# Where the second projection of the keys' latent stands among the indexer's query tiles

## The chip, the cores and the metric

The program runs on one core of one Trainium2 chip. The metric is the time of one execution on the device, in microseconds (us), less is better. A core has a matmul engine (TensorE, in the profile PE, with its weight loads as PEld), a vector engine (VectorE, DVE), a scalar engine (ScalarE, ACT), GpSimd (POOL), and a queue (SyncE, SP) from which most transfers are issued. Each engine works through its own instructions strictly in the order in which they stand in the program, and waits for the others by semaphores.

## The reference

Two layers of a transformer block with 512 tokens and a width of 1024. A layer projects its input with one matrix of 13 x 128 columns and then runs two kinds of attention: eight heads of latent attention (MLA), whose keys and values come out of a 256 wide latent, and eight heads of sparse attention (DSA), where an indexer picks 128 keys for each query. After that come the output projection, a layer norm, a mixture of 16 experts with two per token, and another layer norm.

```python
proj = h @ w_in
qa, kva, kr, dq, dk, dv, iq, ik, iw = jnp.split(proj, SPLIT_POINTS, axis=-1)
# MLA: the keys' latent
c_kv = rms_norm(kva, kv_norm_g)
k_nope = (c_kv @ w_uk).reshape(B, T, MLA_HEADS, MLA_NOPE)
v = (c_kv @ w_uv).reshape(B, T, MLA_HEADS, MLA_V)
# DSA: the indexer
rel = jax.nn.relu(jnp.einsum('bthd,bsd->bths', iqb, ik) * (IDX_DIM ** -0.5))
score = jnp.einsum('bths,bth->bts', rel, iwb).astype(jnp.float32)
score = jnp.where(key_idx[None, None, :] <= tq[None, :, None], score, -jnp.inf)
_, sel = lax.top_k(score, n_keep)
```

## The kernel before, in words

The kernel takes the 13 column tiles of the first projection in a fixed order (S, two for the indexer's queries IQ, DKV, two for the keys' latent KVA, three for QA, four for DQ). Each tile is a `proj`: 24 matmuls of 128x512 into one PSUM bank, since the numbers are split into a high and a low part and three products are summed (`project`, L264 to L271). Before a tile can be multiplied its weights are split: ScalarE writes the high part (L163), GpSimd or VectorE the low part (L164). The banks for these products, and for scores, come from a ring of four named `mm`.

`latents(i)` (L333 to L336) is the projection of one of the two KVA tiles. ScalarE then reads its bank twice, once for the scaled latent `kvg` (L335) and once for its squares `sqk` (L336). GpSimd adds the two squares (L381, at the `anchor`), and TensorE sums them over the columns with four small matmuls (L418).

The indexer (L339 to L377) runs over the query tiles i = 1, 2, 3 (tile 0 needs no choice). For each of eight heads it does one matmul of the queries with the keys (L347), of 256, 384 or 512 columns for i = 1, 2, 3, then on ScalarE a relu that frees the bank (L352), then on VectorE one multiply-add into `acc` (L355 for head 0, L358 for heads 1 to 7). The queries of heads 0 to 3 and of heads 4 to 7 lie in two tiles `iq`, which come back through DRAM (`big<-iqd`). When all heads of a tile are summed, VectorE takes the 128 largest of each row in 16 rounds of a maximum of eight (L365) and a replacement (L366), then compares (L368) and writes the distance mask `dd` (L372). This top-k is given a lower priority (`LOWER`), so that the scheduler puts the rounds between other work of VectorE.

`KVA_AT` (L338) tells ahead of which (query tile, head) of the indexer the two `latents` are emitted; `proj` of the QA and DQ tiles follow the indexer. A scheduler orders the instructions of each engine from the order of emission, priorities and its own estimates; the order is fixed when the program is built. After QA and DQ come the norm factors (L422, L427, L434), the values (L457), and the attention heads in the groups of `HEADS`, "m0 m1d0 m2d1 m3d2 d3": m is a pair of latent heads, d a pair of sparse heads. A head is: four scores on TensorE (L545 for m, L558 and L559 for d), minimum with the mask on VectorE (L490), exponential on ScalarE (L492), reciprocal and scaling on VectorE (L494, L498), transposes on TensorE (L502) with copies on ScalarE (L504), and the product with the values (L511). A sparse head's fourth query tile needs the mask that tile i = 3 of the indexer makes. `queries` makes the queries of a pair of latent heads (24 matmuls named `mm<-qg,hl`, L220 to L223, then L530 on VectorE), `latent` the keys of a pair (six matmuls `mm<-big,hl`, then L536 and L537).

Of the kernel before, what the change touches and what calls it, by code (L numbers as in the profile page):

```python
# [95 lines left out]
def block_kernel(ctx, tc, xT0, x0, win, wqk, wuv, wo, gvec, lnp, rw, rb, wgu, wdn, consts, angles, stripd, rowsd, out):  # L96
# [56 lines left out]
    def ps(tag):  # L153
        return psp.tile([128, 512], F32, name=tag, bufs={"mm": 4, "tr": 2, "pv": 2}[tag])
# [76 lines left out]
    def attention(l, xh, xl, wraw, first, rest, x_dram):  # L231
# [101 lines left out]
        def latents(i):  # L333
            p = proj(T_KVA + i)
            nc.scalar.activation(kvg[i], p, AF.Copy, scale=gv[:, l, 3 + i:4 + i])  # L335
            nc.scalar.activation(sqk[i], p, AF.Square)  # L336

        KVA_AT = ((1,0), (3,0))  # L338
        for i in range(1, NT):  # L339
            n = 128 * (i + 1)  # L340
            acc, work = u4p("aw")
# [1 line left out]
            for h in range(8):  # L343
                if (i, h) in KVA_AT:
                    latents(KVA_AT.index((i, h)))
                p = ps("mm")
# [31 lines left out]
        for i in range(2):  # L378
            if KVA_AT[i] is None:
                latents(i)  # L380
# [1039 lines left out]
    for l in range(L):  # L1420
        r, pre = attention(l, xh, xl, wraw, ws, rest, src)
        y = experts(l, r, pre)
        wraw = pre["win"]
        new = combine(l, r, *y, pre["x1"], wraw)
        if l + 1 < L:
            xh, xl, rest, ws = new
        src = x1d
# [59 lines left out]
```

## Time and profile before

| what | us |
|---|---|
| median of 3 runs | 1191.95 (1191.82 to 1192.46) |
| the profiled execution, its own time | 1192.57 |
| its span, first to last instruction | 1190.8 |
| busy: PE, PEld, DVE, ACT, POOL | 1142.6, 893.5, 1020.2, 791.2, 285.6 |
| first layer, indexer from the first KVA tile's end to the first QA tile | 40.25 to 56.64 |
| second layer, the same | 628.24 to 647.35 |

Times within the trace count from the start of the span. The profiled execution lies 0.62 us above the median, and 1.77 us of its time lie outside the span. Over the whole span TensorE is busy 96% of the time and VectorE 86%, but those are means over stages with different limits: from about 42 to 146 us and again from about 637 to 737 us VectorE is the engine without gaps. Ends of matmuls are modelled in the profile, so a busy TensorE isn't always one at its peak; the weight loads beside it (PEld) tell more.

### The profile page before, as it was taken

To read this page: it belongs to the slowest core of one execution; us is meant where nothing else is said; L and a number is where in the kernel's file an instruction comes from. 1 tells how busy PE (TensorE), PEld (TensorE's weight loads), DVE (VectorE), ACT (ScalarE), POOL (GpSimd) and SP (SyncE) were. 2 spreads that over 40 slices of the span, in tenths; PEclk is the share of its full clock that TensorE was granted. 3 is DMA by queue.
4 is the path that set the end of the run, shared out by engine and by line. 5 is a ranking of instruction groups with operands and counts; after the bars stand their busy time and mean duration, and the time that the engine had idled before them with its cause. 6 is when DMAs were issued, how large, how long until landed. Compare 5 with 4: busy or idle time off the path is not lost. (4 is left out here: it accounts for less than half of the span.)

```text
span 1190.8 us, 16760 instructions
## 1 busy us (share of the span) xinstructions
PE 1142.6 (96%) x5705; PEld 893.5 (75%) x5705; DVE 1020.2 (86%) x1858; ACT 791.2 (66%) x1253; POOL 285.6 (24%) x236
## 2 busy tenths in 40 slices
PE   8999899999999999999998998999999999999996
PEld 6786555788788888887696765567887888888873
DVE  4599968399999999988957999774999999999898
ACT  4633668445888888887445346683468888888882
POOL 2345233121111111111132453422212111112011
PEclk9999999999999999999998999999999999999998
DMA  7626104366999999994735170144669999999841
GB/s 263 183 82 203 71 1 142 142 236 247 405 395 393 393 386 375 383 333 176 289 104 151 58 260 2 39 138 155 242 270 397 400 391 389 392 378 375 328 189 71
DMA packets 57547, 292.50 MB, mean 246 GB/s; under 512 B 10309, under 2 KB 14149, under 8 KB 29040
## 3 DMA queue, kind: packets, MB, share of 16 engines
q1 hardware_dynamic: 47664, 270.48, 60.9%
q0 software_dynamic: 8352, 15.66, 3.5%
q10 hardware_dynamic: 1440, 5.24, 1.1%
q8 instruction: 46, 0.75, 0.2%
q14 instruction: 45, 0.37, 0.1%
HBM read 267.96 MB, written 33.03 MB: 253 GB/s over the span
## 5 line engine op out<-in xcount | busy, mean ns | idle before, releaser
L163 ACT CAST hl<-big 128x1024 fp32r<-128x1024 f32 x438 | 457.4, 1054 | 123.0 <-PE mm L1065 51.3
L164 DVE TENSOR_TENSOR hl<-big,hl 128x1024 fp32r<-128x1024 f32 x403 | 483.7, 1227 | 47.7 <-ACT hl L163 41.7
L1064 PE MATMUL mm<-hl,xh 128*128 128x512 f32 x504 | 207.2, 411 | 0.6 <-ACT hl L163 0.6
L1065 PE MATMUL mm<-hl,xh 128*128 128x512 f32 x504 | 197.3, 392 | 0.0
L1086 PE MATMUL pv<-hl,hT 128*128 128x512 f32 x720 | 169.9, 390 | 0.1
L1086 PEld LDWEIGHTS pv<-hl,hT 128*128 128x128 f32 x720 | 134.7, 188 | 28.7 <-DVE hl L164 1.0
L271 PE MATMUL mm<-big,hl 128*128 128x512 f32 (+1 forms) x624 | 140.3, 384 | 2.4 <-ACT big L163 1.7
L271 PEld LDWEIGHTS mm<-big,hl 128*128 128x128 f32 x624 | 112.9, 193 | 27.7 <-ACT hl L163 2.3
L164 POOL TENSOR_TENSOR hl<-big,hl 128x1024 fp32r<-128x1024 f32 x35 | 86.5, 2476 | 133.7 <-ACT hl L163 118.2
L1028 POOL DMA_INDIRECT xg<-xdr,ii x30 | 54.0, 1800 | 268.9 <-DVE ii L1042 242.4
L1064 PEld LDWEIGHTS mm<-hl,xh 128*128 128x128 f32 x504 | 94.8, 188 | 16.8 <-ACT hl L163 1.1
L1065 PEld LDWEIGHTS mm<-hl,xh 128*128 128x128 f32 x504 | 95.1, 189 | 15.7
L1065 PE MATMUL mm<-hl,xl 128*128 128x512 f32 x252 | 98.9, 392 | 0.0
L1064 PE MATMUL mm<-hl,xl 128*128 128x512 f32 x252 | 98.8, 392 | 0.0
L635 PE MATMUL mm<-hl,big 128*128 128x512 f32 x384 | 93.4, 396 | 0.0
L492 ACT ACTIVATE P<-P,mn 128x128 f32<-128x128 f32 (+3 forms) x128 | 71.9, 569 | 17.2 <-DVE mn L490 14.8
L635 PEld LDWEIGHTS mm<-hl,big 128*128 128x128 f32 x384 | 70.8, 188 | 13.6
L1106 POOL DMA_INDIRECT ydr<-y,ii x28 | 30.2, 1079 | 189.4 <-ACT y L1102 117.5
L504 ACT COPY big<-tr 128x512 f32<-128x512 f32 (+3 forms) x128 | 49.8, 432 | 36.5 <-PE tr L502 35.6
L502 PE MATMUL tr<-cn,P 128*128 128x128 f32 x320 | 61.9, 293 | 9.1 <-DVE P L498 8.3
L502 PEld LDWEIGHTS tr<-cn,P 128*128 128x128 f32 x320 | 36.2, 141 | 41.7 <-ACT big L504 17.1
L572 POOL TENSOR_TENSOR mh<-dd,cn 128x256 f32<-128x256 f32 (+2 forms) x64 | 44.6, 718 | 64.9 <-DVE mn L490 39.5
(277 smaller groups left out, 1816.7 us busy)
## 6 DMA issues: line engine op xcount, KB each, us to landing
big<-wgu SPq DMA_DIRECT2D x128, 1024.0 KB, 8.2
big<-wdn SPq DMA_DIRECT2D x64, 1024.0 KB, 7.9
big<-win SPq DMA_DIRECT2D x10, 1024.0 KB, 5.4
ydr<-zz SPq DMA_DIRECT2D x2, 4096.0 KB
big<-wo SPq DMA_DIRECT2D x8, 1024.0 KB, 14.8
big<-ydr SPq DMA_DIRECT2D x8, 1024.0 KB, 12.7
big<-wqk SPq DMA_DIRECT2D x4, 1024.0 KB, 5.1
big<-dq SPq DMA_DIRECT2D x32, 128.0 KB, 2.3
```

The source lines that it names most:

```text
L163: i = nc.scalar.copy(hi, src).ins
L164: last_lo[0] = (eng or nc.vector).tensor_sub(lo, src, hi.bitcast(F32)).ins
L271: nc.tensor.matmul(p[:, ts], w[j == 1][:, k * 128:(k + 1) * 128], x, start=(j + k == 0), stop=(j == end and k == 7))
L492: nc.scalar.activation(e, e, AF.Exp, bias=mn[:, i:i + 1], scale=-1.0, accum_out=su[:, i:i + 1])
L502: nc.tensor.transpose(p[:, (i - kb) * 128:(i - kb + 1) * 128], P[:, PO[i] + kb * 128:PO[i] + (kb + 1) * 128], ident)
L504: copies.append(nc.scalar.copy(pt[kb], p[:, :512 - 128 * kb]).ins)
L572: last_mask[0] = nc.gpsimd.tensor_tensor(m[:, c:c + w], dd, C("slope", h, h + 1).to_broadcast([128, w]), op=OP.mult)
L635: R["pe"] = nc.tensor.matmul(pp[t][i], x, w[:, i * 512:(i + 1) * 512], start=first, stop=last).ins
L1028: return nc.gpsimd.indirect_dma_start(out=st[e]["xg"], out_offset=None, in_=xdr[l], in_offset=bass.IndirectOffsetOnAxis(ap=st[e]["ii"][:, ...
L1064: nc.tensor.matmul(pg, x, w[:, :512], start=(k == 0 and x is a and w is wh), stop=last)
L1065: nc.tensor.matmul(pu, x, w[:, 512:], start=(k == 0 and x is a and w is wh), stop=last)
L1086: nc.tensor.matmul(py[i], x, w[:, i * 512:(i + 1) * 512], start=(k == 0 and x is a and w is wh), stop=last)
```

## The change

The second `latents` is emitted ahead of head 4 of query tile 1 in place of head 0 of query tile 3. It holds for both layers. Nothing else differs in the source; the scheduler then orders much of the first half of the attention anew.

```diff
-        KVA_AT = ((1,0), (3,0))
+        KVA_AT = ((1, 0), (1, 4))
```

TensorE in the first layer, from the first KVA tile (24 matmuls L271) to the QA and DQ tiles; L347 are the indexer's scores and L418 the sums over the latent's squares:

```order
 L271 MATMUL mm<-big,hl 128x512 x24
-L347 MATMUL mm<-ik,big 128x256 x8
-L347 MATMUL mm<-ik,big 128x384 x8
+L347 MATMUL mm<-ik,big 128x256 x4
 L271 MATMUL mm<-big,hl 128x512 x24
-L347 MATMUL mm<-ik,big 128x512 x5
-L418 MATMUL pv<-cn,sqk 128x1 x4
-L347 MATMUL mm<-ik,big 128x512 x3
+L347 MATMUL mm<-ik,big 128x256 x4
+L347 MATMUL mm<-ik,big 128x384
+L418 MATMUL pv<-cn,sqk 128x1
```

The second 24 matmuls stood behind the scores of two query tiles and now stand behind four scores of the first; the sums L418 follow among the scores of tile 2.

The same place in the second layer:

```order
-L347 MATMUL mm<-ik,big 128x256 x8
+L347 MATMUL mm<-ik,big 128x256 x4
+L271 MATMUL mm<-big,hl 128x512 x24
+L418 MATMUL pv<-cn,sqk 128x1 x4
+L347 MATMUL mm<-ik,big 128x256 x4
 L347 MATMUL mm<-ik,big 128x384 x8
-L271 MATMUL mm<-big,hl 128x512 x24
```

Here all four sums L418 come directly behind the 24 matmuls, and the scores of heads 4 to 7 behind those.

VectorE in the first layer, in the attention, around the end of the last top-k, whose compare is L368 and whose masks are the two L372 (`mh` marks the first pair of sparse heads). Before:

```order
L490 ISA P,mn<-mm,mh 128x384
L490 ISA mn 128x1
L365 MAX m_640<-aw 128x8
L366 MATCH_REPLACE aw<-m_640,aw 128x512
L368 TENSOR_TENSOR aw<-aw 128x512
L530 TENSOR_TENSOR q<-mm,ct 128x512
L372 SCALAR_TENSOR_TENSOR dd<-aw,at 128x384
L372 SCALAR_TENSOR_TENSOR dd_325<-aw,at 128x128
L530 TENSOR_TENSOR q<-mm,ct 128x512
L490 ISA P,mn<-mm,mh 128x512
```

After the change:

```order
L490 ISA P,mn<-mm,mh 128x384
L490 ISA mn 128x1
L365 MAX m_637<-aw 128x8
L366 MATCH_REPLACE aw<-m_637,aw 128x512
L365 MAX m_640<-aw 128x8
L366 MATCH_REPLACE aw<-m_640,aw 128x512
L368 TENSOR_TENSOR aw<-aw 128x512
L372 SCALAR_TENSOR_TENSOR dd<-aw,at 128x384
L372 SCALAR_TENSOR_TENSOR dd_325<-aw,at 128x128
L490 ISA P,mn<-mm,mh 128x512
```

The L490 at the top is the first sparse head's in the first listing and the second sparse head's in the second: the three L490 of that second head, four L490 of a further latent head, both L530 and one L164 now stand ahead of the two L372.

TensorE in the first layer, where both orders have just issued the second sparse head's scores (L558, L559); L502 are transposes of finished heads:

```order
 L558 MATMUL mm<-kk,big 128x512
-L502 MATMUL tr<-cn,P 128x128
 L559 MATMUL mm<-kk,big 128x512
-L502 MATMUL tr<-cn,P 128x128 x6
 L220 MATMUL mm<-big,hl 128x512
 L221 MATMUL mm<-big,hl 128x512
 L220 MATMUL mm<-big,hl 128x512
-L502 MATMUL tr<-cn,P 128x128 x3
+L221 MATMUL mm<-big,hl 128x512
+L223 MATMUL mm<-big,hl 128x512 x2
+L545 MATMUL mm<-ke,q 128x128
+L545 MATMUL mm<-ke,q 128x256
```

The six matmuls of the next `latent` and its four scores L545 have moved ahead of the first transposes of the group with a sparse head.

## Rows read from the trace of the kernel before

**Rows 1.** Busy time by stretch: us, then busy us of PE, PEld, DVE, ACT, POOL.

```profile
46.60:134.70 88.10, 83.08 (x364) 62.83 (x364) 85.52 (x213) 37.83 (x75) 34.97 (x20) 0.98 0.40 132
637.20:725.70 88.50, 82.88 (x363) 62.61 (x363) 85.72 (x213) 38.17 (x76) 32.40 (x19) 0.98 0.39 131
57.00:87.00 30.00, 30.00 (x146) 25.05 (x145) 29.09 (x57) 10.96 (x16) 12.87 (x5) 1.00 0.25 89
148.30:215.00 66.70, 63.61 (x345) 40.13 (x345) 49.73 (x168) 49.54 (x154) 22.90 (x35) 0.97 0.25 85
739.40:806.00 66.60, 63.52 (x350) 39.97 (x350) 50.03 (x168) 49.95 (x156) 22.98 (x35) 1.00 0.27 89
```

**Rows 2.** Timeline of TensorE, first layer: start, us, instruction, count [idle before, releaser].

```profile
41.68 4.42 PE L347 MATMUL mm<-ik,big 128*128 128x256 f32 x13 [0.92 <-ACT sqk L336]
45.90 6.41 PE L271 MATMUL mm<-big,hl 128*128 128x512 f32 x24
...
56.64 27.55 PE L271 MATMUL mm<-big,hl 128*128 128x512 f32 x120
...
94.17 3.00 PE L434 MATMUL pv<-dg,cn 128*128 128x512 f32 x4 [1.80 <-POOL dg L427]
```

**Rows 3.** The same, second layer.

```profile
628.98 0.86 PE L347 MATMUL mm<-ik,big 128*128 128x256 f32 x4 [0.79 <-DMA big<-iqd]
632.84 4.12 PE L347 MATMUL mm<-ik,big 128*128 128x256 f32 x12 [2.99 <-DMA big<-iqd]
...
647.35 27.48 PE L271 MATMUL mm<-big,hl 128*128 128x512 f32 x120
```

**Rows 4.** Timeline of ScalarE, both layers.

```profile
41.52 5.38 ACT L352 ACTIVATE big<-mm 128x256 f32<-128x256 f32 x16
...
52.34 0.69 ACT L335 ACTIVATE kvg<-mm,gv 128x512 f32<-128x512 f32 x1 [4.52 <-PE mm L271]
52.93 0.59 ACT L336 ACTIVATE sqk<-mm 128x512 f32<-128x512 f32 x1
53.41 2.55 ACT L352 ACTIVATE big<-mm 128x512 f32<-128x512 f32 x5
...
630.24 1.22 ACT L352 ACTIVATE big<-mm 128x256 f32<-128x256 f32 x4
```

**Rows 5.** Timeline of GpSimd, first layer, the sum of squares.

```profile
53.60 1.28 POOL L381 TENSOR_TENSOR sqk<-sqk 128x512 f32<-128x512 f32 x1 [3.24 <-ACT sqk L336]
```

**Rows 6.** Timeline of VectorE, the first tile's sums and top-k, both layers.

```profile
42.53 4.01 DVE L358 SCALAR_TENSOR_TENSOR aw<-big,iwt,aw 128x256 f32<-128x256 f32 x7
...
633.15 4.03 DVE L358 SCALAR_TENSOR_TENSOR aw<-big,iwt,aw 128x256 f32<-128x256 f32 x7
```

**Rows 7.** Timeline of VectorE, first layer, in the attention.

```profile
112.62 0.68 DVE L530 TENSOR_TENSOR q<-mm,ct 128x512 f32<-128x512 f32 x1
...
141.96 0.75 DVE L372 SCALAR_TENSOR_TENSOR dd<-aw,at 128x384 f32<-128x384 f32 x2
...
144.61 0.29 DVE L490 CUSTOM_DVE_ANT_0 P<-mm,at 128x128 f32<-128x128 f32 x1
...
146.56 3.63 DVE L498 TENSOR_SCALAR P<-P,rc 128x128 f32<-128x128 f32 x4
...
153.15 1.22 DVE L164 TENSOR_TENSOR hl<-big,hl 128x1024 fp32r<-128x1024 f32 x1
```

**Rows 8.** Timeline of TensorE: the first head's scores, the first sparse transposes (both layers).

```profile
114.95 2.43 PE L545 MATMUL mm<-ke,q 128*128 128x128 f32 x8 [0.67 <-ACT ke L536]
...
148.26 0.30 PE L502 MATMUL tr<-cn,P 128*128 128x128 f32 x1 [1.07 <-DVE P L498]
739.40 0.30 PE L502 MATMUL tr<-cn,P 128*128 128x128 f32 x1 [1.07 <-DVE P L498]
```

**Rows 9.** Granted clock (the number behind POOL's count) in two stretches.

```profile
44.00:48.00 4.00, 4.00 (x12) 3.04 (x12) 3.46 (x9) 3.82 (x9) 0.05 (x1) 0.57 0.38 158
94.00:99.00 5.00, 4.83 (x10) 2.66 (x11) 4.79 (x13) 0.00 (x0) 5.00 (x4) 0.66 0.57 131
```

## The prediction

> **What bounds the kernel now.** I read the busy time by stretch first, since the page's means (TensorE 96%, VectorE 86%) hide which engine ends last where the change is. From 46.6 to 134.7 us in the first layer VectorE is busy 85.52 of 88.10 us, and the second layer repeats it with 85.72 of 88.50 [rows 1]. The 3% missing are the small gaps between an instruction and the one that needs its result. TensorE is nearly as busy there, but VectorE's time cannot be shortened: it is the three top-k of the indexer, its sums, and the first heads of the attention, one behind the other. The timelines then show where that stretch begins and where it is paid. It begins when the last sum of query tile 1 ends, at 42.53 + 4.01 = 46.5 us, and 633.15 + 4.03 = 637.2 us in the second layer [rows 6]; the first top-k follows at once. It is paid where TensorE wants to transpose the first group with a sparse head: it waits 1.07 us for VectorE's L498 there, in both layers [rows 8], and that L498 is behind the last top-k, whose masks (L372) end at 142.7 us [rows 7]. So until about 146 us the top-k chain on VectorE sets the time, and TensorE has little to spare at its end. What delays the first top-k delays everything after it, as far as no later slack takes it up.
>
> **The change, first layer.** It removes nothing and adds nothing. 24 matmuls move from behind 16 scores to behind four.
>
> TensorE's first part gets better. Head 3's score needs the bank that `sqk` frees, and runs at 41.7 as before [rows 2]. The projection needs head 0's bank, which ScalarE frees 0.4 us after 41.52 [rows 4], so it starts at 42.0. At 27.55/120 = 0.23 us a matmul [rows 2] it takes 5.5 us plus 0.2 for the last to drain: 47.7.
>
> Heads 4 to 7 come out later, and that is the core of it. ScalarE must read the projection's bank twice first, 0.59 to the next start and 0.48 more [rows 4]: head 4's relu starts at 48.8 and ends at 49.2. Four sums on VectorE at 4.01/7 = 0.57 [rows 6] end at 51.5. The first top-k starts at 51.5 instead of 46.5: VectorE is **4.9 us** late (it idles between head 3 and head 4).
>
> The QA projection is not earlier. The column sums L418 wait for `sqk` and 1.28 us of GpSimd [rows 5], so until 50.3, and hold up the scores of tile 2 behind them. The relus of tiles 2 and 3 run at 0.34 for the mean of 256 and 384 columns (5.38/16) and 0.51 for 512 [rows 4], and with two stops of half a microsecond the bank for QA is free at about 56.8, where it was 56.64 [rows 2]. Worth nothing either way.
>
> Later TensorE can gain some: it now waits 1.80 us for the norm factors at 94.17 [rows 2], and the granted clock falls there to 0.66 of full on the mean, half (1.2 of 2.4 GHz) for some 3.4 of 5 us [rows 9]. In the new order VectorE reaches L422 with six rounds of the second top-k left for later, so L434 starts some 0.6 us earlier, with the projection before it ending just then. I give this up to 2.2 us and cost it at nothing: the first head's scores at 114.95 [rows 8] need L530, which VectorE reaches at 112.62 before [rows 7] and by my count of its new order at 112.6 after. VectorE is the cover; without it, see the second rival.
>
> **Second layer.** Heads 0 to 3 wait for the queries' transfer until 628.98, and heads 4 to 7 for its other half until 632.84, 2.99 us of idle TensorE [rows 3]. The projection now goes into that gap. It needs head 0's bank, freed at 630.24 + 0.43 [rows 4], so it runs from 630.7 to 636.4. But here all four sums L418 stand ahead of head 4. They need kvg, sqk (1.2), GpSimd (1.3) and take 1.05 themselves as eight records of 0.13: 639.9. Head 4's relu ends at 640.6, the four sums on VectorE at 642.9, where it was 637.2: **5.7 us** late. The QA projection starts at about 647.0 (647.35 [rows 3]).
>
> **What the lateness is worth at the end.** VectorE takes the same path from there, packed, and the new order puts more ahead of the masks: four L490 of another latent head, 146.56 - 144.61 = 1.95 with its issue gaps, three of the second sparse head, some 1.0, and one L164 of 1.2 [rows 7], together 4.1 us. So L372 ends at 142.7 + 4.9 + 4.1 = 151.7, and the first sparse transposes run at some 157 in place of 148.26. TensorE in turn has six matmuls (1.4) and four scores (2.0 of the 2.43 [rows 8] to the next start) behind it that used to come later, 3.4 us. What stays late then is 4.9 us for VectorE and between 3.7 and 5.6 for TensorE. I take 4.9, and 5.7 in the second layer: 10.6.
>
> What the second half of the attention gives back is the open term. TensorE is idle for 66.70 - 63.61 = 3.1 us from 148.3 to 215 and 3.1 in the second layer [rows 1]. Nothing of it (all waits are links of the same chain of scores, minimum, exponential, scaling, transposes) and all of it are the two ends; I take half, 1.5 a layer, since the waits there are split between that chain and banks. The stage behind it is busy matmuls and hides nothing.
>
> The clock is costed at nothing: now the second KVA projection takes 6.41 us for 5.5, at a mean clock of 0.57 [rows 2, 9]; it will run at full speed and QA's start, behind 9 us of sparse scores, at half. That trades 0.9 for 0.9.
>
> **The sum.** 4.9 + 5.7 - 1.5 - 1.5 = 7.6 us on the profiled 1192.57: 1200.2; its time is 0.6 above the median, so **1199.5**. With all slack given back 4.4 us (1196.4), with nothing given back, 1.0 more a layer (half of 5.6 - 3.7) and 0.9 of clock on top 13.5 (1205.5).
>
> The transfers stay: SP's order is the same, and the load that `proj` issues only asks for its buffer earlier. GpSimd's order up to the masks is the same.
>
> **Rivals.**
> *The second half wins it all back.* TensorE's busy share of 148.3 to 215 is 95%, but its weight loads fill 40.13 of 66.70 us, 60%, where a packed stretch has 25.05 of 30, 84% [rows 1]. If that is room, 66.70 x (1 - 0.60/0.84) = 19 us a layer could take up the 4.9 and 5.7, and the time is 1192, within 0.2%. Against it: ScalarE and VectorE are each at 75% there too, all three in one loop, and room inside a chain of waits is not a place to catch up. The Trainium skill has a rule for it (Perfetto Trace Analysis, Identifying the Most-Contended Engine): busy matmuls are a bad measure of headroom, weight-load busy time is a good one. By that rule alone this rival would be the forecast; the 1.07 us wait at the stretch's start [rows 8] is what I set against it.
>
> *Faster.* If VectorE's lateness is not what TensorE waits for, the other effects show: 2.2 us at L434 in the first layer, 0.3 at QA in the second and up to 2.1 of the filled wait, 2.99 less 0.9 that stays, so 2.5 to 4.6 and about 1188.5. This decides if the masks at 142.7 have 5 us to spare. Rows 8 speak against that, since TensorE already waits there. The skill has a sentence for this side too (the same page, Optimization Strategy): stages with different limiting engines may gain from being interleaved, which is what the change does.
>
> *Worse.* The first and second sparse head's fourth scores each keep one of four `mm` banks until the last mask. With two banks left, the next head's scores (2.0) and its L490 (1.95) no longer overlap: 4 us more in each layer, 1207.5.
>
> That the change moves less than it says is ruled out by the listings.
>
> **Chances.** Forecast 0.72, worse 0.06, won back 0.12, faster 0.10. Of "won back" I count a quarter as slower by over 0.2% (2.4 us, about what a measurement can tell from no change). So slower 0.81, same 0.09, faster 0.10. The range from 1192.0 to 1205.5 leaves out faster, half of "won back" and most of worse.
>
> **What would show it.** First top-k of tile 1 at 51.5 and 642.9; VectorE idle for about 5 us before it; QA's start within 0.5 us of before; L372 of tile 3 at about 151 and 743; the wait of the first sparse transposes for L498 grown to several us; the attention's end 3 to 4 us later in each layer. I am wrong if those masks come late and the output projection still starts on time, or if VectorE gets through its order without being packed.

## The result, and the profile after

The changed kernel takes 1213.18 us, the median of 4 runs (1212.89 to 1213.56); the kernel before, run beside it, 1192.2 (1191.82 to 1194.26). The ratio is 1.0171, with a 95% interval of 1.0159 to 1.0183: **slower by 1.7%, some 21 us**. The direction was forecast, the size was not: 1199.5 was predicted, and 1205.5 was the end of the range.

| what | before | after |
|---|---|---|
| span of the profiled execution | 1190.8 | 1211.4 |
| busy: PE, DVE | 1142.6, 1020.2 | 1154.6, 1020.6 |
| first top-k starts, first layer | 46.6 | 52.4 |
| the last masks L372 start, first layer | 142.0 | 155.1 |
| first output projection L635, first layer | 211.0 | 220.4 |
| last output projection L635, second layer | 858.5 | 879.1 |

VectorE does the same work in the same time (1020.2 and 1020.6 us busy), so the loss is waiting. The start of the output projection, which follows the attention, tells where it arose. Before, and then after (line view of L635: shortest, median and longest in ns, first and last start in us):

```profile
L635 PE MATMUL mm<-hl,big x384: 387/389/483, 211.0 to 858.5; 128*128 128x512 f32 x192
```

```profile
L635 PE MATMUL mm<-hl,big x384: 387/389/484, 220.4 to 879.1; 128*128 128x512 f32 x192
```

The first layer's attention ends 9.4 us later and the second's 20.6: 9.4 and 11.2 us a layer, and nothing elsewhere.

TensorE after, first layer, which answers to [rows 2] (timeline: start, us, instruction, count, idle before it and its releaser):

```profile
41.99 5.73 PE L271 MATMUL mm<-big,hl 128*128 128x512 f32 x24
47.56 0.51 PE L347 MATMUL mm<-ik,big 128*128 128x256 f32 x3
...
50.34 0.38 PE L418 MATMUL pv<-cn,sqk 128*128 128x1 f32 x2 [0.63 <-POOL sqk L381]
...
57.62 2.76 PE L271 MATMUL mm<-big,hl 128*128 128x512 f32 x11
```

VectorE there, which answers to [rows 6]:

```profile
42.56 1.66 DVE L358 SCALAR_TENSOR_TENSOR aw<-big,iwt,aw 128x256 f32<-128x256 f32 x3
49.24 3.09 DVE L358 SCALAR_TENSOR_TENSOR aw<-big,iwt,aw 128x256 f32<-128x256 f32 x4 [5.02 <-ACT big L352]
52.37 0.43 DVE L365 MAX8 m<-aw 128x8 f32<-128x256 f32 x1
```

and GpSimd, which answers to [rows 5]:

```profile
49.01 1.27 POOL L381 TENSOR_TENSOR sqk<-sqk 128x512 f32<-128x512 f32 x1 [2.48 <-ACT sqk L336]
```

The projection runs from 42.0 to 47.7, to the tenth where it was forecast, and VectorE idles 5.02 us for head 4. But the four sums take 3.09 us, where the same four take 2.25 in the second layer (below). The first top-k is 5.8 us late.

The second layer, TensorE (as [rows 3]) and VectorE:

```profile
638.38 0.92 PE L347 MATMUL mm<-ik,big 128*128 128x256 f32 x4 [0.73 <-DMA big<-iqd]
640.12 5.75 PE L271 MATMUL mm<-big,hl 128*128 128x512 f32 x24 [0.83 <-ACT big L352]
648.48 1.87 PE L418 MATMUL pv<-cn,sqk 128*128 128x1 f32 x8 [2.60 <-POOL sqk L381]
650.21 7.45 PE L347 MATMUL mm<-ik,big 128*128 128x256 f32 x20
```

```profile
651.22 2.25 DVE L358 SCALAR_TENSOR_TENSOR aw<-big,iwt,aw 128x256 f32<-128x256 f32 x4 [6.91 <-ACT big L352]
653.51 0.43 DVE L365 MAX8 m<-aw 128x8 f32<-128x256 f32 x1
```

Less the 9.4 that the layer starts late (638.38 against 628.98 in [rows 3]) the top-k starts at 644.1, 6.9 us late. The sums L418 wait for GpSimd as forecast, but take 1.87 us where 1.05 were counted, since TensorE's clock is at half for part of it (columns: stretch, us, then busy us of PE, PEld, DVE, ACT, POOL, granted clock, DMA share, GB/s):

```profile
646.00:652.00 6.00, 3.52 (x14) 3.39 (x15) 0.67 (x2) 3.21 (x8) 3.57 (x2) 0.69 0.00 0
```

From the top-k on VectorE is busy 86.11 of 91.20 us, 94%, against 85.52 of 88.10, 97%, in [rows 1]: nearly packed as before, with some more gaps.

```profile
52.30:143.50 91.20, 85.81 (x371) 64.82 (x371) 86.11 (x218) 41.17 (x90) 31.92 (x20) 0.95 0.39 127
```

Where it is paid, VectorE and then TensorE, first layer (as [rows 7] and [rows 8]):

```profile
155.05 0.76 DVE L372 SCALAR_TENSOR_TENSOR dd<-aw,at 128x384 f32<-128x384 f32 x2
156.90 0.69 DVE L490 CUSTOM_DVE_ANT_0 P<-mm,mh 128x512 f32<-128x512 f32 x1 [1.09 <-POOL mh L572]
```

```profile
150.60 0.51 PE L558 MATMUL mm<-kk,big 128*128 128x512 f32 x1 [0.98 <-DVE mn L490]
...
153.39 1.30 PE L545 MATMUL mm<-ke,q 128*128 128x128 f32 x4 [0.67 <-ACT ke L536]
157.66 3.35 PE L545 MATMUL mm<-ke,q 128*128 128x384 f32 x4 [2.96 <-DVE mn L490]
160.80 1.70 PE L502 MATMUL tr<-cn,P 128*128 128x128 f32 x7
```

The last masks come 13.1 us late (9.0 were forecast). 5.8 of it is the late start. The other 7.3 lie on VectorE's way, where 4.1 were counted: one more L530 stands ahead of the masks (0.7 us, in no term of the sum), a compare lasts 1.4 longer (below), and VectorE idles 1.1 more. TensorE stands 2.96 us with a score of a latent head until VectorE's L490 of a sparse head gives a bank back.

### The profile page after: what moved, and what is told of

The parts are those of the page before. It is cut to its first block, busy times and chain, and to the rows that moved or that the text cites. A ratio compares the mean times of both kernels' runs of the same rounds, so it can differ in the third digit from the quotient of the medians.

```text
span 1211.4 us, 16754 instructions
## 1 busy us (share of the span) xinstructions
PE 1154.6 (95%) x5705; PEld 901.6 (74%) x5705; DVE 1020.6 (84%) x1858; ACT 791.2 (65%) x1253; POOL 282.2 (23%) x236
## 5 line engine op out<-in xcount | busy, mean ns | idle before, releaser
L164 DVE TENSOR_TENSOR hl<-big,hl 128x1024 fp32r<-128x1024 f32 x403 | 484.3, 1228 | 48.0 <-ACT hl L163 41.7
L271 PE MATMUL mm<-big,hl 128*128 128x512 f32 (+1 forms) x624 | 142.3, 388 | 3.3 <-ACT big L163 1.4
L271 PEld LDWEIGHTS mm<-big,hl 128*128 128x128 f32 x624 | 114.4, 196 | 28.7 <-ACT hl L163 2.6
L164 POOL TENSOR_TENSOR hl<-big,hl 128x1024 fp32r<-128x1024 f32 x35 | 85.8, 2454 | 139.6 <-ACT hl L163 125.5
L635 PE MATMUL mm<-hl,big 128*128 128x512 f32 x384 | 93.4, 396 | 0.0
L635 PEld LDWEIGHTS mm<-hl,big 128*128 128x128 f32 x384 | 70.8, 188 | 13.6
L502 PEld LDWEIGHTS tr<-cn,P 128*128 128x128 f32 x320 | 37.7, 145 | 40.8 <-ACT big L504 22.0
L502 PE MATMUL tr<-cn,P 128*128 128x128 f32 x320 | 61.1, 297 | 5.7 <-DVE P L498 4.5
```

What stands on the lines that cost most here:

```text
L164: last_lo[0] = (eng or nc.vector).tensor_sub(lo, src, hi.bitcast(F32)).ins
L271: nc.tensor.matmul(p[:, ts], w[j == 1][:, k * 128:(k + 1) * 128], x, start=(j + k == 0), stop=(j == end and k == 7))
L502: nc.tensor.transpose(p[:, (i - kb) * 128:(i - kb + 1) * 128], P[:, PO[i] + kb * 128:PO[i] + (kb + 1) * 128], ident)
L635: R["pe"] = nc.tensor.matmul(pp[t][i], x, w[:, i * 512:(i + 1) * 512], start=first, stop=last).ins
```

## Experiments

The theories, as the texts below number them: (1) the loss is VectorE's late first top-k, passed on with the waits and the order behind it; (2) the projection's new place costs on TensorE by itself; (3) only the attention's new order costs; (4) the lateness one to one plus a fixed price of the new order. Each ratio is to the kernel before, run in the same session on the same chip (medians of 1192.4 to 1194.7).

**Late, without the move.** On the kernel before:

```diff
-            for _ in range(16):
+            for _ in range(22 if i == 1 else 16):
```

> The kernel before, with 22 rounds in place of 16 in the top-k of query tile 1 (so the masks of that tile are other ones). A round takes 0.985 us on VectorE in the trace of before, so everything behind that top-k is 5.9 us late in each layer, while both projections of the keys' latent stay where they were; the first half of the attention comes out in the order of the changed kernel. Theory 1 (the change costs what VectorE's late start costs, through the waits and the order behind it): about 20 us in all, 1210 to 1214. Theory 2 (the place of the projection on TensorE costs by itself: early column sums, banks, clock): VectorE's 5.9 a layer passes on at most one to one, 1204 or less. Theory 3 (only the new order in the attention costs, 8 us in all): 1200.

1214.38 us, ratio 1.0166 [1.0149, 1.0183]. With both projections in their old place and VectorE 5.9 us late the whole loss is there. The attention's order on VectorE and, but for a few transposes, on TensorE is then the change's. Theory 2 falls; the lateness and the order are not told apart here.

**The move, without the lateness.** On the changed kernel, `range(9 if i == 1 else 16)` in the same line.

> The changed kernel, with 9 rounds in place of 16 in the top-k of query tile 1 (the masks of that tile are other ones). 7 rounds of 0.985 us less give VectorE 6.9 us back in each layer, where the change took 5.8 and 6.9; the attention then comes out in the order of the kernel before. Theory 1: the time of before, 1190 to 1193. Theory 2: TensorE's place still costs, so over 1198. Theory 3: the order is that of before, so 1190 to 1193 as well.

1193.9, ratio 0.9999 [0.9990, 1.0009]. With VectorE's time given back the projection may stand where the change puts it: nothing is lost. The order is then that of before, but for a few transposes.

**The masks ahead of the other work.** On the changed kernel:

```diff
-                m8 = sm.tile([128, 8], F32, name="m8")
+                tc.cur_priority += -1500 if (i, _) == (3, 8) else 0; m8 = sm.tile([128, 8], F32, name="m8")
```

> The changed kernel, with the last 8 rounds, the compare and the masks of query tile 3 at the priority of the work around them: on VectorE the two L372 then stand ahead of the four L490 of the further latent head and of two L530, as before the change; nothing is left out. The first top-k still starts 5.8 and 6.9 us late. Theory 1 with a one-to-one price for lateness and the rest (about 8 us in all) for the work put ahead of the masks: 1204 to 1206. If the lateness costs all 20 whatever the order: 1211 to 1214. Theory 3 (the order alone): 1192 to 1196.

1209.63, ratio 1.0137 [1.0115, 1.0159]; its span is 16.5 us over before's, the change's 20.6. Of the 16.5, 1.3 us lie ahead of the change: the first projection ends at 41.68 us in this execution and at 40.41 in that of before. So the order counts for a part, 4 to 5 us where some 8 were expected.

**The second projection behind tile 1.**

```diff
-        KVA_AT = ((1,0), (3,0))
+        KVA_AT = ((1,0), (2,0))
```

> The second projection ahead of head 0 of query tile 2, so behind all eight scores of tile 1, in both layers. VectorE's first top-k is then on time (46.5 and about 637 us), and the sums of tile 2 wait behind it anyway. Theory 1: within 2 us of before, 1190 to 1194. Theory 2 (the early column sums and banks, which come early here as well): 1198 or more.

1201.43, ratio 1.0060 [1.0043, 1.0077]: a miss, and it led to a cost that the prediction had not listed. TensorE hands tile 1's scores over in time, but a sum of VectorE lasts 2.63 us where its neighbours take 0.48, beside a split of weights on GpSimd:

```profile
44.81 2.63 DVE L358 SCALAR_TENSOR_TENSOR aw<-big,iwt,aw 128x256 f32<-128x256 f32 x1
```

```profile
44.76 2.40 POOL L164 TENSOR_TENSOR hl<-big,hl 128x1024 fp32r<-128x1024 f32 x1 [5.91 <-DVE aw L358]
```

That is 2.1 us of this run's loss, which is 8.8 by the spans and 7.2 by the ratio. In the second layer the first top-k starts only 0.1 us late and the last masks 0.6, and still 4.1 us are lost there. The attention stands in a third order in this run. A scaling of VectorE ahead of the first transposes is stretched too, in both layers, beside a split that runs from 149.68 to 152.03 us in the first; it loses 0.8 us more than its like in the kernel before:

```profile
149.72 2.46 DVE L498 TENSOR_SCALAR P<-P,rc 128x256 f32<-128x256 f32 x1
```

What the rest is made of stays open.

The kernel before has a stretched sum beside a split in tile 2's sums:

```profile
64.02 2.72 POOL L164 TENSOR_TENSOR hl<-big,hl 128x1024 fp32r<-128x1024 f32 x1 [2.60 <-ACT hl L163]
64.40 2.76 DVE L358 SCALAR_TENSOR_TENSOR aw<-big,iwt,aw 128x384 f32<-128x384 f32 x1
```

and the changed one at a compare of the second top-k, while the replacement beside the same split keeps its 0.67 us. VectorE, then GpSimd:

```profile
110.69 0.67 DVE L366 MATCH_REPLACE8 aw<-m,aw 128x512 f32<-128x512 f32 x1
111.29 1.92 DVE L368 TENSOR_TENSOR aw<-aw 128x384 f32<-128x384 f32 x1
```

```profile
110.39 2.40 POOL L164 TENSOR_TENSOR hl<-big,hl 128x1024 fp32r<-128x1024 f32 x1 [2.83 <-ACT hl L163]
```

VectorE's op with two tensors from SBUF ends 0.3 to 0.4 us after the GpSimd op in all three; the replacement doesn't mind it. The 0.84 us that the four sums of heads 4 to 7 lost above (3.09 less 2.25) are the same thing, beside L381. The Trainium skill states this (SBUF — State Buffer, Who interferes with whom): a VectorE instruction with two SBUF inputs contends with a GpSimd instruction that reads SBUF, the lock is exclusive, and the order of issue decides which of the two waits. The traces agree: in all three the GpSimd op starts first, by 0.05 to 0.9 us.

**GpSimd's split in four pieces**, in the kernel before and in the changed one, all other instructions in their order:

```diff
-        last_lo[0] = (eng or nc.vector).tensor_sub(lo, src, hi.bitcast(F32)).ins
+        for o in range(0, 1024, 256) if eng is nc.gpsimd and lo.shape[-1] == 1024 else (None,): c = slice(None) if o is None else slice(o, o + 256); last_lo[0] = (eng or nc.vector).tensor_sub(lo[:, c], src[:, c], hi[:, c].bitcast(F32)).ins
```

> The kernel before; GpSimd's split of a weight granule (L164, 128x1024, 2.40 us) is cut into four pieces of 256 columns, with the order of all other instructions left as it was. In the trace of before, two sums L358 of query tile 2 that lie beside such a split take 2.75 us where the others take 0.61 to 0.74, so 4.3 us are lost on VectorE in the first layer, and 6.2 with a stretched L355 in the second. Theory 1a (an op of VectorE that reads two tensors waits for the whole op that GpSimd has in progress, so that shorter pieces give back part of it, and VectorE's lateness is passed on): 2 to 6 us faster, 1186 to 1190. Rival (the two take turns piece by piece, so the sum of the waits stays): within 2 us of before. If VectorE's lost time isn't passed on: within 2 us as well, but with short L358.

> The same cut of GpSimd's split in the changed kernel, whose stretched ops on VectorE lose 6.5 us in the first layer and 7.9 in the second, 2.2 and 1.6 more than before. Theory 1a: 4 to 9 us faster than the change, 1204 to 1209, and 2 to 4 us less between this and the cut kernel before than the 20.5 between the change and before, so 17 to 19. Rival: 1211 to 1214.

Before, cut: 1190.81, ratio 0.9981 [0.9972, 0.9991], 1.6 us faster by the medians and 2.3 by the ratio, so on the border between theory 1a's range and the rival's. Changed, cut: 1209.76, ratio 1.0160 [1.0134, 1.0186], between the two ranges; the distance between the cut kernels is 19.0 us. In a row of sums VectorE and GpSimd take turns, and four pieces cost nearly as much as one. VectorE, then GpSimd, in the cut kernel before:

```profile
64.75 4.40 DVE L358 SCALAR_TENSOR_TENSOR aw<-big,iwt,aw 128x384 f32<-128x384 f32 x4
```

```profile
64.50 4.10 POOL L164 TENSOR_TENSOR hl<-big,hl 128x256 fp32r<-128x256 f32 x4 [2.17 <-ACT hl L163]
```

So in the sums little is gained. In the first layer of the cut kernel before, the last masks even come 0.8 us later, and its gain arises right behind them: the first group's scaling L498, for which the transposes wait 1.07 us in [rows 8], is itself stretched by a split in the kernel before. VectorE, then GpSimd:

```profile
146.56 1.56 DVE L498 TENSOR_SCALAR P<-P,rc 128x128 f32<-128x128 f32 x1
```

```profile
145.66 2.37 POOL L164 TENSOR_TENSOR hl<-big,hl 128x1024 fp32r<-128x1024 f32 x1
```

Cut, this scaling takes 0.58 us; the 1.07 us wait is gone, TensorE's granted clock stays at 1.00 where it was 0.69 from 150.5 to 155.0 us, and the attention ends 0.85 us earlier than before. Of the change's 20.5 us the cut takes away 1.5, which is inside the intervals (some 3 us).

**The first projection later.** On the kernel before, `KVA_AT = ((2, 0), (3, 0))`:

> The kernel before, with the first projection of the latent behind the scores of query tile 1 (ahead of head 0 of tile 2); the second stays ahead of tile 3. In the first layer TensorE is free for the scores at 34.7 and the queries' two halves land at about 36 and 38, so the first top-k can start near 42 in place of 46.6; the first projection runs 4 us later. In the second layer the scores wait for the same transfer as before (628.98), without the projection to fill the time, so the top-k starts at 636 to 637 and TensorE is 5 us late. Theory 1 (VectorE's start sets the end): 4 to 7 us faster in the first layer, 0 to 1 in the second, 1185 to 1189. Rival (TensorE's 4 to 5 us, through the projections that the attention needs, set it): 0 to 10 us slower.

1195.43, ratio 1.0026 [1.0015, 1.0038]: theory 1's number missed, the rival's came. The last masks of the first layer end at 133.6 us, 9.1 earlier than before, and the output projection still starts 2.6 later: early masks alone win nothing. The order is another here too. The second half of the queries lands at 42.0, not at 38, so the top-k gains 1.3 us only; and the waits leave TensorE at half clock for a part of the projection behind them, 7.22 us for 24 matmuls that take 5.73 at full clock above. Timeline, then windows:

```profile
38.39 0.71 PE L347 MATMUL mm<-ik,big 128*128 128x256 f32 x4 [2.46 <-DMA big<-iqd]
42.00 1.19 PE L347 MATMUL mm<-ik,big 128*128 128x256 f32 x4 [2.90 <-DMA big<-iqd]
43.03 7.22 PE L271 MATMUL mm<-big,hl 128*128 128x512 f32 x24
```

```profile
38.40:43.00 4.60, 1.70 (x8) 1.42 (x8) 2.41 (x4) 1.62 (x6) 1.47 (x1) 0.61 1.06 294
43.00:50.20 7.20, 7.20 (x26) 5.82 (x26) 6.52 (x19) 0.80 (x3) 0.00 (x0) 0.77 0.63 200
```

**Lateness in the old order.** On the kernel before, `KVA_AT = ((1, 4), (3, 0))`; behind the indexer every engine keeps the order of before:

> The kernel before, with the first projection between heads 3 and 4 of query tile 1 and the second where it was; the order of everything behind the indexer is that of before, word for word. In the second layer heads 4 to 7 then come behind a projection, as in the change, and the first top-k is some 5 us late; in the first layer heads 0 to 3 run in TensorE's wait and the top-k is within 1 us of before. Theory 1: the second layer is 5 to 8 us longer, the first within 1, so 1197 to 1201. If only the new order of the attention makes the loss (theory 3): within 2 us of before.

1198.44, ratio 1.0050 [1.0032, 1.0067]. The first top-k starts at 49.68 and 643.44:

```profile
49.68 0.43 DVE L365 MAX8 m<-aw 128x8 f32<-128x256 f32 x1
...
643.44 0.43 DVE L365 MAX8 m<-aw 128x8 f32<-128x256 f32 x1
```

```profile
L635 PE MATMUL mm<-hl,big x384: 387/389/481, 213.0 to 864.3; 128*128 128x512 f32 x192
```

In the first layer it is 3.1 us late and the output projection 2.0. In the second, less those 2.0, it is 4.2 late, and the end 3.8. The first layer's lateness was not expected (the queries land at 37.7, and the projection behind that wait took 7.36 us); what counts is that here less comes out than goes in, 5.8 for 7.3. In the first layer the shift falls from 3.1 to 2.0 at one place, the matmuls behind the first group's transposes, which ran at a mean clock of 0.69 in the kernel before (150.5 to 155.0 us) and at 1.00 here; from there to the output projection every transpose and product of the attention keeps its 2.0.

**The new order, with little lateness.** On the changed kernel, `range(12 if i == 1 else 16)`:

> The changed kernel, with 12 rounds in place of 16 in the top-k of query tile 1 (the masks of that tile are other ones). VectorE gets 4 rounds of 0.985 us back in each layer, so of the 5.8 and 6.9 us of lateness 1.9 and 2.9 stay; at the last masks the order is still the change's (44 L490 records ahead of the last L372, 30 before the change). Theory 4 (the change's loss is the lateness, about one to one, plus a fixed price of the order that the scheduler made, some 3.5 to 4.2 us a layer): 1.9 + 2.9 + 7.7, 1203 to 1206. Theory 1 with a loss in proportion (1.6 us for each of lateness): 1199 to 1201. If the order is free: 1196 to 1198.

1206.17, ratio 1.0109 [1.0092, 1.0126]. Theory 4's range by the ratio (1192.2 x 1.0109 = 1205.2), far from the two others. So the order has a price of its own. (The attention's order is the change's but for some 30 instructions of TensorE and 20 of VectorE a layer.)

**The sparse heads later**, in the kernel before and in the changed one:

```diff
-HEADS = "m0 m1d0 m2d1 m3d2 d3"
+HEADS = "m0 m1 m2d0 m3d1 d2 d3"
```

> The kernel before, with the attention's groups as m0, m1, m2 d0, m3 d1, d2, d3 in place of m0, m1 d0, m2 d1, m3 d2, d3: the first sparse pair, which needs the last masks, comes one latent pair later. If the last masks bound the attention in the kernel before: 2 to 6 us faster, 1186 to 1190. If the groups with one pair alone (m1, d2, d3), which have no second pair to fill the waits of the chain of scores, minimum, exponential and transposes, cost more: 3 to 10 us slower, 1195 to 1202.

> The same groups in the changed kernel. Theory 4: the late masks are then needed a latent pair later (at least the 13 us by which they are late), so the distance between the change and the kernel before, 20.5 us in the old groups, shrinks to 0 to 12 in these. If lateness is passed on wherever the masks are needed: it stays at 17 to 21.

Before: 1190.28, ratio 0.9977 [0.9967, 0.9987]; changed: 1200.41, ratio 1.0061 [1.0044, 1.0078]. Where the last masks are needed later, the change costs 10.1 us in place of 20.5, within theory 4's range, and the kernel before gains 3.0. The first top-k of the changed one is 5.8 and 6.7 us later than that of the other here, 12.4 us for a loss of 10.1: in these groups no price of the order is left over, but most of the lateness still is passed on.

**Both gains together**, in the kernel before:

> The two edits that came out faster than the kernel before, together: the first sparse pair one latent pair later, and GpSimd's split of a weight granule in four pieces; both latents where they were before. If the two gains (1.9 and 1.6 us against the before of their own session by the medians, 2 to 3 for the first by its profiled span) add up: 3 to 4.5 us faster than before, 1188 to 1190. If they overlap, because both buy VectorE time ahead of the last masks, which are no longer waited for: 1.5 to 2.5 us.

1190.34 beside 1194.65, ratio 0.9966 [0.9951, 0.9981]: 4 us faster than before, and than the change by 2%. (The 1.9 in that text was misread; the medians of that session give 3.0.) The gains nearly add up, within an interval of 2.3 to 5.9 us.

**What the runs say together.** Lateness is how much later VectorE's first top-k starts than in before, both layers added, each counted from the first projection's end where that did not move; of it 0.985 us is taken off for each round left out, or put on for each added. The loss is the span's, against 1190.8; the last column takes one for one off it.

| kernel | order of the attention | lateness | loss | loss over lateness |
|---|---|---|---|---|
| the change | the change's | 5.8 + 6.9 | 20.6 | 7.9 |
| late, without the move | the change's, but for a few transposes | 5.9 + 5.9 | 21.5 | 9.7 |
| 12 rounds | the change's around the masks | 1.8 + 3.9 | 12.3 | 6.6 |
| masks first | another | 5.8 + 6.8 | 16.5, less the 1.3 ahead | 2.6 |
| second projection behind tile 1 | another | 2.2 + 0.1 | 8.8 | 6.5 |
| first projection later | another | -1.3 - 3.8 | 3.1 | 8.2 |
| 9 rounds | before's, but for a few transposes | -1.1 - 0.1 | 0.0 | 1.2 |
| first projection split off | before's | 3.1 + 4.2 | 5.8 | -1.5 |

Taken one to one, the change is 12.7 us of lateness and some 8 of order; the three kernels with its order, or nearly it, give 6.6 to 9.7 for the order. The cleanest pair is "first projection split off" against before, where every engine keeps one order: 0.8 us of loss for each of lateness. The two rows with the projections elsewhere show that another order can cost 6 to 8 us with a top-k that is hardly late or early (in the one with the first projection later, TensorE's work is late as well).

The waits of TensorE from 135 to 200 us show what the order does (who waited for whom: total us, times, longest). Before:

```profile
PE tr L502 <- DVE P L498: 3.9, 9, 1.1
PE mm L558 <- DVE mn L490: 0.2, 1, 0.2
```

After:

```profile
PE mm L545 <- DVE mn L490: 3.0, 1, 3.0
PE mm L558 <- DVE mn L490: 1.9, 3, 1.0
PE tr L502 <- DVE P L498: 1.0, 3, 0.4
```

Masks first:

```profile
PE tr L502 <- DVE P L498: 4.7, 9, 1.5
PE mm L220 <- DVE mn L490: 1.9, 2, 1.3
```

12 rounds:

```profile
PE mm L558 <- DVE mn L490: 1.9, 3, 1.0
PE tr L502 <- DVE P L498: 1.2, 4, 0.4
```

Score banks held for VectorE's minimum: 0.2 us before, 4.9 after. With the 12 rounds the long wait is gone, and so is the lowered clock behind it (0.66 on the mean; 0.50, half, from 158 to 161 us). The same stretch, before, after and with 12 rounds:

```profile
155.00:165.00 10.00, 9.89 (x61) 6.21 (x57) 4.76 (x18) 7.41 (x22) 0.20 (x1) 1.00 0.00 1
```

```profile
155.00:165.00 10.00, 6.88 (x18) 3.43 (x20) 6.85 (x21) 4.38 (x14) 5.34 (x9) 0.66 0.01 2
```

```profile
155.00:165.00 10.00, 9.21 (x46) 5.21 (x46) 6.66 (x25) 7.63 (x23) 2.52 (x5) 1.00 0.01 3
```

Yet 12 rounds still lose 6.6 us over their lateness. So the held banks and the clock are only a part of the order's price; the rest is put down to the order by the table, and in which of its links it lies stays open. More banks for scores were not tried.

## Why the prediction was wrong in size, step by step

**What bounds the kernel.** Right in that VectorE's path from the first top-k to the last masks passes its lateness on: late without the move, the loss is there (1.0166); moved without being late, there is none (0.9999). Both runs also switch the attention's order, so for the order of before alone the 5.8 us for 7.3 tell it. The wait of 1.07 us, which the prediction took for the sign of it, was misread: the scaling waited for lasted 1.56 us in place of 0.28 beside a GpSimd split, and with the split cut the wait is gone though the masks come later.

**The first layer's lateness.** 4.9 forecast, 5.8 measured. The projection, the relu and the wait came as worked out; what was missing is 0.84 us in which the sums collide with GpSimd's L381, an op that the next paragraph had priced and placed at that moment. The trace of before held the sign: tile 2's sums at 1.2 us on the mean in place of 0.6.

**The second layer's.** 5.7 forecast, 6.9 measured: 0.8 of it is the column sums L418 at half clock, the rest the scores behind them.

**QA, L434 and the first scores.** QA starts at 57.6 (56.8 forecast) and L434 no longer waits; behind both VectorE goes on packed, so neither is seen to matter, as said. L530 comes at 114.9 where 112.6 was counted; a part of it is the compare L368 that lost 1.4 us to GpSimd.

**What the lateness is worth at the end: the step that failed.** It said that L372 ends at 151.7, that the work now ahead of the masks is work not done later, and so that "what stays late then is 4.9 us for VectorE and between 3.7 and 5.6 for TensorE" (the 3.7 has no working there). L372 ended at 155.8, and 9.4 us stayed late, 11.2 in the second layer. The exchange is not neutral: in the new order TensorE stands before held banks (4.9 us in place of 0.2) and then runs at half clock for a while, and beyond the lateness some 4 us a layer are lost. How much of the 4 each of these links makes is not shown. The sign that was to show the forecast, a longer wait of the first transposes for L498, did not come: that wait fell from 3.9 us to 1.0, and TensorE waited for banks instead.

**What the second half gives back.** 1.5 a layer was forecast; no run shows it. In the old order 1.1 and 0.4 came back, the 1.1 at the first group's matmuls by the clock and none of it in the rest of the first layer's attention; in the new one nothing did. So the low end that the prediction had named, nothing, came out.

**The clock.** It was to trade 0.9 for 0.9. The second projection did run at full clock (5.73 us for 6.41), but QA's start did too: from 57.6 to 62.0 us the granted clock is 0.99, and the half clock fell on the scores ahead of it (0.50 from 51.9 to 57.6). The 0.57 of [rows 9] was misread: it is that of 44 to 48 us, half of them scores; over the projection itself, 45.9 to 52.3, the clock was 0.88. What the clock cost, at half behind the held banks, the prediction had put at nothing.

**The rivals.** "Won back" is out: in the old order too the stretch returned at most 1.1 us. The Trainium skill says that TensorE's headroom is to be judged by weight-load busy time and not by matmul busy time (Perfetto Trace Analysis, Identifying the Most-Contended Engine); the 19 us a layer that the prediction worked out by it for this rival were not there to catch up with. "Faster" is out: of 3.1 us by which the masks were late in the old order 2.0 came out at the end. "Worse" named one link that the traces show, sparse heads that keep banks, and its price of 4 us a layer is near the order's 7.9 in all. That the two are so near is in part luck: with 12 rounds the long wait for a bank is gone and 6.6 us remain. It was given 6 in 100 and left outside the sum, although the listing of the new order already showed its condition: a further latent head's scores issued behind the second sparse head's, with the masks later still. As a term of the sum (7.6 + 8) it would have given 1207.5, and without the 3 given back 1210.5.

## What to carry to other kernels

When an engine that is packed up to a deadline starts late, price the start, and then, separately, the order that the scheduler makes of it; a row of the new order that puts work between a held buffer and what frees it is a term of the sum, not a remote rival. To tell such causes apart, give the engine its lost time back in another way (fewer rounds) or take it away without the change (more rounds). Read the durations, not only the waits: one instruction at three or more times its neighbours' time is a wait that no column of waits shows, and it can be the reason of a wait that is shown, as the 1.07 us here.

## What the runs showed of the hardware

An op of VectorE that reads two tensors from SBUF, started beside a GpSimd op that does too, ended only after it: 2.76 us in place of 0.61 beside one of 2.72, and 1.92 in place of 0.55 at the compare. The scaling L498, which reads one tensor and a number for each row, did the same: 1.56 in place of 0.28, and 2.46 in place of 0.35. A maximum or a replacement of 512 columns beside the same GpSimd op kept its 0.67 to 0.70 us. Cut in four, the GpSimd op took turns with a row of sums, and four sums lasted 4.40 us, where one alone takes 0.61 or 0.74 by its width. TensorE, after waits of 2.46 and 2.90 us, ran the next 24 matmuls in 7.22 us at a mean granted clock of 0.77, against 5.73 at 1.00 without such waits.
